# First tiles of seven normed products taken from x·A before the rstd is known, and one sum instead of four behind the post-norms

## Chip, cores, metric

One Trainium2 chip, one of its cores. The metric is device time in microseconds (us) of one execution. The engines: TensorE (PE in the profile; PEld is its weight load), VectorE (DVE), ScalarE (ACT), GpSimd (POOL) and SyncE (SP), on whose queue nearly all DMAs are issued.

## What is computed

Two model blocks in float32, one after the other, each of two layers, on 256 tokens of 1024 features; block 1 also carries 256 tokens of context through its first layer.

```python
# block 1, layer l (x and the context cx alike; cx is not updated in layer 1)
sh1, sc1, ga1, sh2, sc2, ga2 = split(silu(c) @ w_mod + b_mod, 6)
u = (rmsnorm(x, g_mix) * (1 + sc1) + sh1) @ w_in      # pool | linear attention | attention
x = x + ga1 * (concat([pool, gla, attention]) @ w_out)
x = x + ga2 * (square(relu((rmsnorm(x, g_mlp) * (1 + sc2) + sh2) @ w_up)) @ w_down)
# after both layers: x = rmsnorm(x, g_final)

# block 2, layer l
shift_a, scale_a, gate_a, shift_f, scale_f, gate_f = split(silu(c) @ w_ada + b_ada, 6)
h = rmsnorm(x, g_mix_pre) * (1 + scale_a) + shift_a
x = x + gate_a * rmsnorm(hybrid_mixer(h), g_mix_post)  # three attentions, then @ w_out
h = rmsnorm(x, g_ffn_pre) * (1 + scale_f) + shift_f
x = x + gate_f * rmsnorm((silu(h @ w_gate) * (h @ w_up)) @ w_down, g_ffn_post)
```

rmsnorm multiplies a token by the inverse root of its mean square (the rstd) and by a gain.

## The kernel before

Activations lie with the features on the partitions: `x` is eight tiles ("chunks") of 128 features by 512 columns. In block 1 these are the 256 tokens and the 256 context tokens (T = 512; 256 in layer 1 behind the in-projection); in block 2 the tokens take the first 256 columns and the output `y` of a mixer or feed-forward the others.

**Products.** Every weight is streamed once, in pieces `wraw` (two buffers) on SP's queue. ACT casts a piece to a rounded part `whi` (L135), DVE subtracts to get the rest `wlo` (L136); activations are split in the same way. An output tile of 128 features is a sum of three matmuls a chunk (high by high, high by low, low by high), so a 1024-deep tile is 24 matmuls and a pair of tiles 48. A product is written with one tile after the other, or `by_k`, chunk by chunk over all its tiles, so that it can follow a norm that delivers chunk after chunk. For the first products behind a norm the weights are split ahead (`early`, and `early_act` for two more tiles, `wact`).

**A norm.** ACT squares the chunks, DVE or POOL adds the squares, TensorE sums over the partitions (`st`, matmuls with ones), DVE makes the mean (`ms`, L236), POOL raises it to −1/2 (L237), TensorE transposes the rstd onto all partitions (`bc`). Then `norm_chunk` makes each h chunk: DVE `nt` = x·A·rstd (L295), ACT adds B and rounds (L297, L299), DVE, ACT or POOL make the low part (L300 to L303). A and B come from the modulation vectors.

**Post (block 2).** Behind w_out and behind the feed-forward of layer 0, x + G·r·y is normed at once. `Post.chunk` gathers four sums as the y tiles arrive: of x², of x·G·y, of (G·y)² and of y², with three ACT squares, a DVE product (L1229), a DVE add of 512 columns (L1231) and a POOL add of 512 columns (L1232, DVE for the last tile). Two `pow` steps then give both rstds, one `bc` holds them, and `Post.norm` updates x and makes h. `first_norm` does the like between the blocks.

**Fill.** The modulation vectors are products of their own: 24 or 32 matmuls `pmod` from eight `mraw` DMAs of 512 KB each. `queue_mod` queues them and `pump` emits steps (one DMA, four matmuls, which the profile counts as eight) at a given `pace` per product; a scheduler that orders each engine's instructions ahead of the run puts them where it expects TensorE to wait. `mraw` has two buffers in layer 0 of block 1, four in layer 1, six in block 2. SP's queue is served in order: a DMA that waits for a buffer holds up those behind it.

Of the kernel before, what the change touches and what calls it, by code (L numbers as in the profile page):

```python
# [10 lines left out]
F32 = mybir.dt.float32  # L11
# [9 lines left out]
D = 1024  # L21
# [3 lines left out]
LAG, ADDV, TAIL = 1, (1, 3, 5, 7), 6  # L25
PACE1 = 2, 1
# [4 lines left out]
class K:  # L31
# [6 lines left out]
    # ---------------------------------------------------------------- pools  # L38
# [91 lines left out]
    # ------------------------------------------------------- building blocks  # L130
# [18 lines left out]
    def gemm_a(self, src, nt, h, t0, t1, evac, by_k=False):  # L149
        """src [128, nt*K*128]: output features on partitions, tokens t0:t1 of the chunks h."""  # L150
# [27 lines left out]

    def gemm_half(self, src, h, half, t0, t1, evac):
        """gemm_a for two tiles, over one half of the chunks of h."""  # L180
# [15 lines left out]
    def early(self, src, nt, K_):  # L196
        """The weights of the next product by chunks, ahead of what comes before it."""
# [5 lines left out]
    def early_act(self, src, act):  # L203
        """Two tiles more, kept where the activations are."""
# [7 lines left out]
    def gemm_b(self, src, N, h, tts, evac):  # L212
        """src [128, K*N]: tokens on partitions, one output per token tile of tts."""
# [6 lines left out]
        for tt in tts:  # L220
            t = slice(tt * 128, (tt + 1) * 128)
            p = self.psum("pb")
            o = p[:, :N]
            for k in range(K_):
                hi, lo = gr[k // g]
                w = slice((k % g) * N, (k % g + 1) * N)
                self.mm(o, h[k][:, 0, t], hi[:, w], k == 0, False)
                self.mm(o, h[k][:, 0, t], lo[:, w], False, False)
                self.mm(o, h[k][:, 1, t], hi[:, w], False, k == K_ - 1)
            evac(tt, o)  # L230

    def pow_rstd(self, dst, st, n, tag="smn"):
        """dst = (st / n + eps) ** -0.5"""
# [5 lines left out]
    def exp_rstd(self, dst, st, n, tag="smn"):  # L239
        """The same for many columns, where the table of Exp and Ln is loaded: a step of Newton's makes it exact."""  # L240
# [10 lines left out]
    def rstd_bc(self, groups, T, sets=(6, 1, 1), eng=None):  # L251
# [4 lines left out]
        st = self.psum("st")  # L256
# [22 lines left out]
        bc = self.psum("bc")  # L279
# [4 lines left out]
    def norm_mod(self, T, mod, act, *sets, bc=None):  # L284
        """mod: [(t0, t1, A [128,8], B [128,8])]; the chunks of x * rstd * A + B, split."""
# [20 lines left out]
    def modulation(self, b, l, ss, boot=None):  # L306
        """The vectors ss of layer l of block b, [128, rows, 8] each, a row block of the weights a step."""
# [29 lines left out]
    def pump(self, n=None):  # L337
        """Emit n steps of the queued modulations (all of them: None)."""
# [13 lines left out]
    def gain(self, g, sc, tag):  # L352
        """g * (1 + sc)"""
# [4 lines left out]
    # ---------------------------------------------------------------- block 1  # L358
    def block1(self, top):
        tc, nc, a = self.tc, self.nc, self.a  # L360
        ranges = [(0, 256), (256, 512)]
        for l in range(2):
            T = 512 if l == 0 else 256
            m = lambda s: self.mod(0, l, s)
            with ExitStack() as es:
                self.mrp = es.enter_context(tc.tile_pool(name=f"mrp{l}", bufs=(2, 4)[l], reuse_waits="tile"))
                act = es.enter_context(tc.tile_pool(name=f"act{l}", bufs=10, reuse_waits="tile"))
                if l == 0:
# [7 lines left out]
                else:  # L376
                    self.early(a["w_in_a"][1, 0], 2, 8)
# [3 lines left out]
                h = self.norm_mod(512, [(*ranges[r], A[r], m(0)[:, r]) for r in range(2)], act)  # L381
                with tc.tile_pool(name=f"mix{l}", bufs=1, reuse_waits="tile") as mp:
                    self.queue_mod(0, l, [2, 3, 4], PACE1[l])
                    mix = self.mixers1(l, T, h, act, mp)
# [1034 lines left out]
```

## Time and profile before

| | |
|---|---|
| three executions | 1909.71, 1912.74, 1915.86 us (median 1912.74) |
| profiled execution | span 1926.9 us from its first to its last instruction |
| TensorE busy | 1822.9 us, 95% of the span |
| DVE, ACT, POOL busy | 1077.5, 816.9, 226.9 us |
| mean granted TensorE clock | 0.959 |

The profile is of an execution of its own; its span is already 14.2 us (0.7%) above the median of the others, and it has no time beside the span that the views show. All views below are of that one execution, in us from its first instruction. TensorE's busy time counts overlapping matmuls once, but it also counts fill and matmuls at a low clock as busy.

### The profile page before, as it was taken

What the parts mean: (1) busy time and instruction counts of PE and PEld (TensorE: products, weight loads), DVE (VectorE), ACT (ScalarE), POOL (GpSimd) and SP (SyncE); (2) the same over time, 40 slices, a digit from 0 to 9 for tenths busy, and PEclk for the clock granted to TensorE, in tenths of its full rate; (3) what the DMA queues carried; (4) which work ended last, traced back from release to release, by engine and by line L of the source; (5) the groups of instructions that cost most, each with busy time, mean ns of one, the idle gap of its engine ahead of it and who ended that gap; (6) DMA issues with size and microseconds to landing.
All of it is one profiled execution on the core that took longest, in us unless ns stands there. A gap on an engine that the chain in (4) does not pass through costs nothing. (4 is left out here: it accounts for less than half of the span.)

```text
span 1926.9 us, 31942 instructions
## 1 busy us (share of the span) xinstructions
PE 1822.9 (95%) x12982; PEld 1509.5 (78%) x12982; DVE 1077.5 (56%) x2012; ACT 816.9 (42%) x1563; POOL 226.9 (12%) x253
## 2 busy tenths in 40 slices
PE   5998799999999999989999999998999899989998
PEld 3776446778777787865799986986999868869997
DVE  3237865544444546277666564466544754575555
ACT  3343433433222224544454444464444445544443
POOL 2024410100000002051100012012000230030000
PEclk9998978999999999999999998997999989989999
DMA  8422321232333234424655676345666654254553
GB/s 324 165 90 77 122 84 34 99 109 88 120 131 113 106 131 151 162 94 138 214 206 193 212 262 224 111 127 191 205 212 218 208 200 168 78 175 163 187 177 130
DMA packets 66211, 298.75 MB, mean 155 GB/s; under 512 B 9552, under 2 KB 13572, under 8 KB 45328
## 3 DMA queue, kind: packets, MB, share of 16 engines
q1 hardware_dynamic: 65168, 295.65, 45.0%
q8 instruction: 102, 1.67, 0.3%
q0 software_dynamic: 464, 1.05, 0.2%
q14 instruction: 45, 0.37, 0.1%
q10 hardware_dynamic: 432, 0.01, 0.0%
HBM read 295.63 MB, written 1.05 MB: 154 GB/s over the span
## 5 line engine op out<-in xcount | busy, mean ns | idle before, releaser
L132 PE MATMUL pa<-h,whi 128*128 128x256 f32 (+1 forms) x3008 | 660.6, 315 | 10.5 <-ACT h L299 9.3
L136 DVE TENSOR_TENSOR wlo<-wraw,whi 128x1024 fp32r<-128x1024 f32 (+4 forms) x406 | 448.4, 1105 | 365.6 <-ACT whi L135 362.5
L135 ACT CAST whi<-wraw 128x1024 fp32r<-128x1024 f32 (+4 forms) x406 | 380.3, 937 | 608.1 <-PE pa L132 576.7
L132 PEld LDWEIGHTS pa<-h,whi 128*128 128x128 f32 x3008 | 496.0, 192 | 61.3 <-ACT h L299 11.9
L132 PE MATMUL pa<-h,wlo 128*128 128x256 f32 (+1 forms) x1504 | 469.8, 312 | 0.0
L132 PE MATMUL pa<-hid,whi 128*128 128x256 f32 (+1 forms) x1728 | 381.4, 317 | 0.3
L132 PEld LDWEIGHTS pa<-hid,whi 128*128 128x128 f32 x1728 | 284.1, 190 | 29.4 <-issue 4.1
L132 PEld LDWEIGHTS pa<-h,wlo 128*128 128x128 f32 x1504 | 289.4, 192 | 18.4 <-DVE wlo L136 1.2
L132 PE MATMUL pa<-hid,wlo 128*128 128x256 f32 (+1 forms) x864 | 273.4, 316 | 2.3 <-DVE wlo L136 2.3
L132 PEld LDWEIGHTS pa<-hid,wlo 128*128 128x128 f32 x864 | 163.8, 190 | 14.5 <-DVE wlo L136 3.2
L392 DVE SCALAR_TENSOR_TENSOR x<-pa,mod,x 128x256 f32<-128x256 f32 x184 | 82.3, 479 | 109.0 <-PE pa L132 108.9
L132 PE MATMUL pmod<-mraw,cp 128*32 128x256 f32 x1408 | 135.0, 412 | 2.8 <-DMA mraw<-in_w_mod_dram 2.2
L132 PE MATMUL pa<-mixc,whi 128*128 128x256 f32 (+1 forms) x512 | 118.6, 321 | 1.9 <-ACT sq L1228 1.9
L132 PEld LDWEIGHTS pa<-mixc,whi 128*128 128x128 f32 x512 | 84.3, 190 | 18.7 <-issue 3.8
L132 PE MATMUL pb<-whi,h 128*128 128x256 f32 (+2 forms) x480 | 98.2, 296 | 0.0
L132 PEld LDWEIGHTS pb<-whi,h 128*128 128x128 f32 x480 | 78.1, 193 | 6.4 <-issue 4.6
L132 PE MATMUL pa<-mixc,wlo 128*128 128x256 f32 (+1 forms) x256 | 80.7, 318 | 0.0
L132 PEld LDWEIGHTS pmod<-mraw,cp 128*32 128x32 f32 x1408 | 39.4, 112 | 48.1 <-issue 22.9
L132 PE MATMUL pb<-wlo,h 128*128 128x256 f32 (+2 forms) x240 | 70.7, 296 | 0.2 <-DVE wlo L136 0.2
L824 DVE TENSOR_REDUCE mx<-pS 128x1 f32<-128x512 f32 (+3 forms) x80 | 45.4, 578 | 37.6 <-PE pS L132 37.3
L135 ACT CAST hid<-rsq 128x512 fp32r<-128x512 f32 (+1 forms) x64 | 32.9, 513 | 71.3 <-DVE rsq L432 71.1
L1232 POOL TENSOR_TENSOR acc<-acc,sq 128x512 f32<-128x512 f32 x18 | 28.4, 1577 | 221.5 <-DVE sq L1229 218.8
(327 smaller groups left out, 2099.3 us busy)
## 6 DMA issues: line engine op xcount, KB each, us to landing
mraw<-in_w_ada_dram SPq DMA_DIRECT2D x96, 512.0 KB, 5.2
wraw<-in_w_gate_up_dram SPq DMA_DIRECT2D x44, 1024.0 KB, 4.9
mraw<-in_w_mod_dram SPq DMA_DIRECT2D x80, 512.0 KB, 4.1
wraw<-in_w_up_dram SPq DMA_DIRECT2D x32, 1024.0 KB, 5.0
wraw<-in_w_down_dram SPq DMA_DIRECT2D x32, 1024.0 KB, 5.0
wraw<-in_w_down_2a_dram SPq DMA_DIRECT2D x16, 1024.0 KB, 5.2
wraw<-in_w_in_2a_dram SPq DMA_DIRECT2D x12, 1024.0 KB, 5.0
wraw<-in_w_in_a_dram SPq DMA_DIRECT2D x10, 1024.0 KB, 7.4
```

Of the source, the lines that this page charges most:

```text
L132: self.last = self.nc.tensor.matmul(out, l, r, start=start, stop=stop, **k).ins
L135: self.nc.scalar.copy(hi, src)
L136: self.nc.vector.tensor_sub(lo, src, hi)
L392: nc.vector.scalar_tensor_tensor(self.x[n][:, s], o[:, s], gate()[:, r, n:n + 1], self.x[n][:, s], op0=ALU.mult, op1=ALU.add)
L824: nc.vector.reduce_max(mx, s, axis=AX.X)
L1232: (nc.vector if k == 7 else nc.gpsimd).tensor_add(self.acc[1], self.acc[1], b)
```

## The change

Seven norms (all but the first of block 1 and the last of block 2) now feed their first tiles twice over. `Lead` makes `xa`, the split of x·A without the rstd, with B as a 257th column (and a column of zeros). `Kernel.lead` multiplies the first two tiles (block 1) or four (block 2) by `xa`, 258 columns wide. The rstd comes later: `lead_out` copies column 256 (W·B) as a bias, multiplies the rest in PSUM by `rr`, the rstd on all partitions, and ACT adds the bias. The remaining tiles still use h, made as before, so the next product becomes the `by_k` one (`i == 1` in the MLP, `i == 2` in the feed-forward, w_in_r in layer 1 of block 1).

`Post` gathers the squares of y alone. x is updated by `update` as soon as that rstd is there, and the norm behind it takes its squares from the new x (`norm`, added up on POOL).

The modulations are queued in another order and at other paces, and `mraw` has three buffers instead of four in layer 1 of block 1.

```diff
-PACE1 = 2, 1
+PACE1 = 3.4, 2.4
...
+    def lead(self, xa, n, by_k=False):
...
+        order = [2, 3, 0, 1][-n:]
+        o = {}
+        for i, j in enumerate(order):
+            o[j] = [self.psum("pS" if i * R + r < 2 else "pa") for r in range(R)]
+        if by_k:
+            steps = [(k, j) for k in range(8) for j in order]
+        else:
+            steps = [(k, j) for j in order for k in range(7)] + [(7, j) for j in order]
...
+            for r in range(R):
+                p = o[j][r][:, :258]
+                self.mm(p, hi, xa[r][:, k, 0], k == 0, False)
+                self.mm(p, hi, xa[r][:, k, 1], False, False)
+                self.mm(p, lo, xa[r][:, k, 0], False, k == 7)
...
+    def lead_out(self, p, rr, dst):
...
+        b = self.small(1, "lb", "smgl")
+        self.nc.vector.tensor_copy(b, p[:, 256:257])
+        self.nc.vector.tensor_mul(dst, p[:, :256], rr)
+        return b
...
-                self.mrp = es.enter_context(tc.tile_pool(name=f"mrp{l}", bufs=(2, 4)[l], reuse_waits="tile"))
+                self.mrp = es.enter_context(tc.tile_pool(name=f"mrp{l}", bufs=(2, 3)[l], reuse_waits="tile"))
...
+            if g == 0:
+                for p in lead:
+                    r = self.etmp(T, "relu")
+                    for i, q in enumerate(p):
+                        t = r[:, i * 256:(i + 1) * 256]
+                        b = self.lead_out(q, rr[:, i * 256:(i + 1) * 256], t)
+                        nc.scalar.activation(t, t, AF.Relu, bias=b)
+                    square(r, hs)
+                h.extend(self.norm_mod(T, mods, act, bc=bc))
...
-        self.gemm_b(a["w_in_r"][l], 288, h, range(4), lambda tt, o: nc.scalar.copy(rkv[:, tt], o))
+        self.gemm_b(a["w_in_r"][l], 288, h, range(4), lambda tt, o: nc.scalar.copy(rkv[:, tt], o), by_k=bool(lead))
...
+                    if f:
+                        f.rstd()
+                    for k in range(8):
+                        if f:
+                            f.update(k)
+                        lead.chunk(k)
+                    return self.lead(lead.xa, 4, by_k=f is not None)
...
+            def norm(mods):
+                bc = self.rstd_bc([(xs, D)], 256, eng=nc.gpsimd, bank="pqt")
+                return bc[:, :256], lambda: self.norm_mod(256, mods, act, bc=bc)
...
+                self.queue_mod(1, l, [2, 3, 4], 1.7)
...
-                    self.queue_mod(1, l, [2])
-                    self.pump()
...
-                self.queue_mod(1, l, [3, 4])
...
-                    self.queue_mod(1, 1, [0, 1], 0.6)
+                    self.queue_mod(1, 1, [0, 1], 0.9)
...
+    def chunk(self, k):
+        nc = self.K.nc
+        for c, (t0, t1, A, _) in zip(self.xa, self.mods):
+            x, g = self.K.x[k][:, t0:t1], A[:, k:k + 1]
+            nc.scalar.activation(c[:, k, 0, :256], x, AF.Copy, scale=g)
+            nc.vector.scalar_tensor_tensor(c[:, k, 1, :256], x, g, c[:, k, 0, :256], op0=ALU.mult, op1=ALU.subtract)
...
-        nc.scalar.activation(b[:, :256], x, AF.Square)
-        nc.scalar.activation(c[:, 256:], y, AF.Square)
-        nc.scalar.activation(c[:, :256], y, AF.Square, scale=G)
-        nc.vector.scalar_tensor_tensor(b[:, 256:], y, G, x, op0=ALU.mult, op1=ALU.mult)
-        if 0 < k < TAIL + 1:
-            nc.vector.tensor_add(self.acc[0], self.acc[0], c)
-            (nc.vector if k == 7 else nc.gpsimd).tensor_add(self.acc[1], self.acc[1], b)
...
+        nc.scalar.activation(q, self.y[k], AF.Square)
+        if k == 0:
+            self.acc = q
+        elif k < 6:
+            nc.vector.tensor_add(self.acc, self.acc, q)
```

How the order of instructions moves is shown at three places; the rows are those of the program, with the counts of its own matmuls (a `pmod` of the program is two in the profile).

First, TensorE at the feed-forward's norm in layer 0 of block 2, before the change: from the last matmul of w_out (`pa<-mixc`) to the first of the feed-forward (`pa<-h`, `pS<-h,wact`).

```order
L132 MATMUL pa<-mixc,wlo 128x256
L132 MATMUL pmod<-mraw,cp_83 32x256 x19
L132 MATMUL st<-ones,acc 128x1 x8
L132 MATMUL pmod<-mraw,cp_83 32x256 x4
L132 MATMUL st<-ones,sq 128x1 x8
L132 MATMUL pmod<-mraw,cp_83 32x256 x4
L1254 MATMUL bc<-c_ident,r_12237 128x128 x4
L132 MATMUL pa<-h,whi 128x256 x2
L132 MATMUL pS<-h,wact 128x256 x2
```

With the change, the same place: to the first matmuls with `xa`, and then from the last of those (row `pqt` on) to the first with h.

```order
L132 MATMUL pa<-mixc,wlo 128x256
L132 MATMUL st<-ones,sq 128x1 x2
L132 MATMUL pmod<-mraw,cp_83 32x256 x7
L359 MATMUL pmt<-c_ident,modr 128x128 x2
L132 MATMUL st<-ones,sq 128x1 x2
L132 MATMUL pmod<-mraw,cp_83 32x256 x20
L1369 MATMUL bc<-c_ident,r_12492 128x128 x2
L132 MATMUL pmod<-mraw,cp_83 32x256 x4
L132 MATMUL pS<-xa_12487,wact 128x258 x2
L132 MATMUL pa<-xa_12487,whi 128x258 x2
```

```order
L132 MATMUL pa<-xa_12487,wlo 128x258
L132 MATMUL pqt<-ones,sq 128x1 x6
L132 MATMUL pmod<-mraw,cp_83 32x256 x4
L316 MATMUL pqt<-c_ident,rs 128x128 x2
L132 MATMUL pmod<-mraw,cp_83 32x256 x3
L359 MATMUL pmt<-c_ident,modr 128x128 x2
L132 MATMUL pmod<-mraw,cp_83 32x256 x20
L132 MATMUL pa<-h,whi 128x256 x2
```

One wait with 27 program matmuls of fill has become two, with 31 and 27; the 96 matmuls with `xa` stand between them, and the sums of the new norm (`pqt`) stand behind the last of them.

Second, DVE at the first norm of block 2 with the change, from the scaling of the first tiles (`cq`, `ck`, L210) to the inputs of the attention's next product (`lt`, `lat`).

```order
L210 TENSOR_TENSOR cq<-pa,rr 128x256 x2
L210 TENSOR_TENSOR ck<-pS,rr 128x256 x2
L330 SCALAR_TENSOR_TENSOR nt<-x,A_10509,bc 128x256 x3
L335 SCALAR_TENSOR_TENSOR h<-nt,mod_8327,h 128x256
L330 SCALAR_TENSOR_TENSOR nt<-x,A_10509,bc 128x256 x3
L335 SCALAR_TENSOR_TENSOR h<-nt,mod_8327,h 128x256
L330 SCALAR_TENSOR_TENSOR nt<-x,A_10509,bc 128x256
...
L335 SCALAR_TENSOR_TENSOR h<-nt,mod_8327,h 128x256
L1060 SCALAR_TENSOR_TENSOR x<-x,c_g_final,bc 128x256 x8
L271 TENSOR_SCALAR ms<-st 128x2 x2
L1166 SCALAR_TENSOR_TENSOR lt<-cq,c_g_q_lat,st 128x256 x2
L1166 SCALAR_TENSOR_TENSOR lt<-ck,c_g_kv_lat,st 128x256
```

The same place before, from the last two h chunks on (L295 and L300 make h, L963 updates x):

```order
L300 SCALAR_TENSOR_TENSOR h<-nt,mod_9194,h 128x256
L295 SCALAR_TENSOR_TENSOR nt<-x,A_10288,bc 128x256
L963 SCALAR_TENSOR_TENSOR x<-x,c_g_final,bc 128x256
L300 SCALAR_TENSOR_TENSOR h<-nt,mod_9194,h 128x256
L963 SCALAR_TENSOR_TENSOR x<-x,c_g_final,bc 128x256 x7
L1209 TENSOR_TENSOR pg<-c_g_mix_post,mod_11868 128x8
L136 TENSOR_TENSOR wlo<-wraw,whi 128x128 x2
L236 TENSOR_SCALAR ms<-st 128x2 x2
L1047 SCALAR_TENSOR_TENSOR lt<-cq,c_g_q_lat,bc 128x256 x2
L1047 SCALAR_TENSOR_TENSOR lt<-ck,c_g_kv_lat,bc 128x256
```

There `cq` and `ck` are written by ACT, and the h chunks and updates of x stand ahead of the product whose tiles they are; now all of them stand between the scaling of those tiles and `ms`, which the next product waits for.

Third, TensorE in layer 1 of block 1 with the change, from the end of w_in_r (`pS<-whi,h`) over the gates of the linear attention (`pg`, from `rkv` over `rT` to `la`) to the next in-projection tiles (`pa<-h`).

```order
L132 MATMUL pS<-whi,h 128x288
L675 MATMUL pg<-c_ident,rkv 32x128 x4
L132 MATMUL pmod<-mraw,cp_82 32x256 x4
L132 MATMUL pg<-wg,rT 128x512
L132 MATMUL pmod<-mraw,cp_82 32x256 x8
L132 MATMUL pg<-wg,rT 128x512
L132 MATMUL pmod<-mraw,cp_82 32x256 x4
L359 MATMUL pmt<-c_ident,modr 128x128 x2
L132 MATMUL pg<-c_UF,la 128x256
L132 MATMUL pg<-c_UF,la 128x128
L132 MATMUL pg<-c_UF,la 128x256
L132 MATMUL pa<-h,whi 128x256 x2
```

Before, the two in-projections `pa<-h` (96 matmuls) came straight behind w_in_r, with `pg<-c_ident,rkv` behind them:

```order
L132 MATMUL pb<-whi,h 128x288 x2
L132 MATMUL pb<-wlo,h 128x288
L132 MATMUL pb<-whi,h 128x288
L132 MATMUL pmod<-mraw,cp_82 32x256 x4
L132 MATMUL pa<-h,whi 128x256 x2
...
L132 MATMUL pa<-h,wlo 128x256
L132 MATMUL pa<-h,whi 128x256 x2
L132 MATMUL pa<-h,wlo 128x256
L600 MATMUL pg<-c_ident,rkv 32x128 x4
L132 MATMUL pmod<-mraw,cp_82 32x256 x4
L132 MATMUL pb<-whi,h 128x256
```

So 96 matmuls that covered the way from `rkv` to `la` now stand behind it.

## Rows read from the trace of the kernel before

**Rows 1.** The page, part 1: busy time, share, instructions.

```profile
PE 1822.9 (95%) x12982; PEld 1509.5 (78%) x12982; DVE 1077.5 (56%) x2012; ACT 816.9 (42%) x1563; POOL 226.9 (12%) x253
```

**Rows 2.** Windows, each from a product's end: PE, PEld, DVE, ACT, POOL, PEclk, DMA.

```profile
740.60:763.20 22.60, 20.71 (x128) 14.13 (x126) 13.77 (x28) 11.52 (x23) 9.09 (x11) 0.92 0.48 174
763.20:779.40 16.20, 16.18 (x130) 13.99 (x128) 3.59 (x6) 4.92 (x8) 0.00 (x0) 1.00 0.71 260
947.60:960.70 13.10, 11.92 (x106) 8.82 (x104) 7.17 (x15) 7.09 (x16) 5.13 (x8) 1.00 0.85 307
1147.00:1183.80 36.80, 34.18 (x274) 23.74 (x272) 17.89 (x49) 16.47 (x40) 6.50 (x9) 0.86 0.57 202
1306.00:1341.30 35.30, 27.27 (x188) 23.19 (x187) 21.04 (x49) 13.59 (x33) 10.28 (x12) 0.71 0.50 184
1537.70:1578.60 40.90, 35.79 (x282) 25.82 (x281) 22.56 (x59) 17.08 (x42) 12.20 (x15) 0.83 0.55 197
1701.10:1735.20 34.10, 25.88 (x188) 22.03 (x186) 21.01 (x49) 13.01 (x31) 10.30 (x12) 0.75 0.32 111
```

**Rows 3.** Of the same windows, the fill (tile pmod) alone.

```profile
1306.00:1341.30 35.30, 4.69 (x54) 1.48 (x54) 0.00 (x0) 0.71 0.50 184
1537.70:1578.60 40.90, 13.67 (x128) 4.49 (x128) 0.83 (x2) 0.83 0.55 197
```

**Rows 4.** Timeline of PE, feed-forward norm of block 2, layer 0: start, us.

```profile
1306.15 2.54 PE L132 MATMUL pmod<-mraw,cp 128*32 128x256 f32 x38
1313.15 3.58 PE L132 MATMUL st<-ones,acc 128*128 128x1 f32 x16 [4.47 <-DVE acc L1231]
1317.67 3.57 PE L132 MATMUL st<-ones,sq 128*128 128x1 f32 x16
1327.15 0.79 PE L132 MATMUL pa<-h,whi 128*128 128x256 f32 x2 [2.43 <-ACT h L299]
```

**Rows 5.** The chain that ended last: start, us, piece.

```profile
1329.23 0.85 PE pS L132 x4
1334.38 0.72 PE pa L132 x6
1383.68 0.57 PE pmod L132 x8
1515.38 4.52 PE pa L132 x36
1562.96 0.72 PE pa L132 x6
1737.82 177.84 PE pa L132 x1482
```

**Rows 6.** Timeline of DVE around three norms.

```profile
1167.92 2.82 DVE L963 SCALAR_TENSOR_TENSOR x<-x,c_g_final,bc 128x256 f32<-128x256 f32 x7
1289.32 1.23 DVE L136 TENSOR_TENSOR wlo<-wraw,whi 128x1024 fp32r<-128x1024 f32 x1 [0.46 <-ACT whi L135]
1296.32 1.45 DVE L1231 TENSOR_TENSOR acc<-acc,sq 128x512 f32<-128x512 f32 x1
1313.42 2.76 DVE L136 TENSOR_TENSOR wact<-wraw,wact 128x256 fp32r<-128x256 f32 x8
1326.08 0.48 DVE L295 SCALAR_TENSOR_TENSOR nt<-x,A,bc 128x256 f32<-128x256 f32 x1 [0.45 <-POOL x L1261]
```

**Rows 7.** Timeline of POOL there.

```profile
1321.52 0.71 POOL L237 TENSOR_TENSOR r<-ms,mhalf 128x2 f32<-128x2 f32 x1 [10.10 <-DVE ms L236]
```

**Rows 8.** Timeline of ACT and DVE, gates of the linear attention, layer 1 of block 1.

```profile
797.27 0.72 ACT L588 ACTIVATE lsg<-lsg,ones 128x512 f32<-128x512 f32 x1
798.03 0.69 DVE L589 SCALAR_TENSOR_TENSOR la<-pg,lsg 128x512 f32<-128x512 f32 x1 [2.60 <-ACT lsg L588]
```

**Rows 9.** Windows as in group 2, mixers of that layer.

```profile
820.00:840.00 20.00, 16.03 (x127) 13.65 (x125) 16.02 (x36) 9.72 (x21) 9.97 (x13) 1.00 0.47 158
```

**Rows 10.** DMA issues between 735 and 800: count, KB, median us to landing.

```profile
mraw<-in_w_mod_dram SPq DMA_DIRECT2D x13, 512.0 KB, 4.7
```

More of the change, by code (lines that the diff above doesn't have):

```diff
@@ L24 @@
 EPS = 1e-6
-LAG, ADDV, TAIL = 1, (1, 3, 5, 7), 6
-PACE1 = 2, 1
+ADDV = 1, 3, 5, 7
+PACE1 = 3.4, 2.4
 GAN = 1152
@@ L396, in block1, with res, ev @@
-                    ev = res(lambda: m(2))
+                self.pump()
+                A = [self.gain(self.g_mlp[:, l], m(4)[:, r], f"A2{r}") for r in range(2)]
+                mods = [(*ranges[r], A[r], m(3)[:, r]) for r in range(T // 256)]
+                def res(gate, lead=None):
+                    def ev(n, o):
+                        for r in range(T // 256):
+                            s = slice(r * 256, r * 256 + 256)
+                            nc.vector.scalar_tensor_tensor(self.x[n][:, s], o[:, s], gate()[:, r, n:n + 1], self.x[n][:, s],
+                                                           op0=ALU.mult, op1=ALU.add)
+                        if lead:
+                            lead.chunk(n)
+                    return ev
@@ L397, in block1 @@
+                with tc.tile_pool(name=f"xup{l}", bufs=1, reuse_waits="tile") as xp:
+                    lead = Lead(self, xp, mods)
+                    ev = res(lambda: m(2), lead)
                     for i in range(4):
@@ L399, in block1 @@
                     del mix
[L400 to L403 removed]
+                    self.early(a["w_up"][l, 0], 2, 8)
+                    o = self.lead(lead.xa, 2)
                 ev = res(lambda: m(5))
@@ L1024, in ffn, with mixers2 @@
         if l == 0:
-            f = Post(self, y, self.f_post[:, l], self.mod(1, l, 5)[:, 0])
+            f = Post(self, y)
         down(2)
         return f
-    def mixers2(self, l, h, act, mp, y):
+    def mixers2(self, l, lead, norm, act, mp, y):
         nc, a = self.nc, self.a
@@ L1037, in mixers2 @@
         ckv, kr = ck[:, 0], ck[:, 1]
-        self.gemm_a(None, 2, h, 0, 256, lambda j, o: nc.scalar.copy((cq if j < 2 else ck)[:, j % 2], o), by_k=True)
+        b2, rest = norm()
+        rr = self.lv(mp, 256, "rr")
+        nc.scalar.copy(rr, b2)
+        for j, p in enumerate(lead):
+            t = (cq if j < 2 else ck)[:, j % 2]
+            b = self.lead_out(p[0], rr, t)
+            nc.scalar.activation(t, t, AF.Identity, bias=b)
+        h = rest()
         mix = [act.tile([128, 2, 256], F32R, name="mixc", tag="act") for _ in range(8)]
@@ L1201, with __init__ @@
 class Post:
[L1205 removed]
+    def __init__(self, K, y):
         self.K, self.y = K, y
[L1207 to L1209 removed]
         self.st = K.psum("st")
[L1211 to L1220 removed]
@@ L1241, in norm @@
[L1241 to L1264 removed]
+        self.acc = None
@@ new lines, in chunk @@
+    def chunk(self, k):
+        K, nc = self.K, self.K.nc
+        q = K.tp.tile([128, 512], F32, name="sq", tag="sq" if k else "ssq", bufs=2)[:, :256]
+        nc.scalar.activation(q, self.y[k], AF.Square)
[3 more added lines that the diff above has]
+            nc.vector.tensor_add(self.acc, self.acc, q)
+        if k >= 5:
+            s = self.acc if k == 5 else q
+            for i in range(2):
+                K.mm(self.st[:, i:i + 1], s[:, i * 128:(i + 1) * 128], K.ones[:, :1], k == 5 and i == 0, k == 7, skip_group_check=True)
@@ new lines, in rstd, with gain, update @@
+    def rstd(self):
+        K, nc = self.K, self.K.nc
+        r = K.small(2, "r1")
+        K.pow_rstd(r, self.st[:, 0:2], D)
+        self.bc = K.psum("bc")
+        for i in range(2):
+            nc.tensor.transpose(self.bc[:, i * 128:(i + 1) * 128], r[:, i:i + 1].to_broadcast([128, 128]), K.ident)
+    def gain(self, g, gate):
+        self.G = self.K.modp.tile([128, 8], F32, name="pg", tag="pg", bufs=2)
+        self.K.nc.vector.tensor_mul(self.G, g, gate)
+    def update(self, k):
+        K, nc = self.K, self.K.nc
+        t = K.tmp(256, "post")
+        x = K.x[k][:, :256]
+        nc.vector.scalar_tensor_tensor(t, self.y[k], self.G[:, k:k + 1], self.bc[:, :256], op0=ALU.mult, op1=ALU.mult)
+        (nc.vector if k in ADDV else nc.gpsimd).tensor_add(x, x, t)
```

228 lines of the change are left out of this document (121 added, 107 removed).

## Prediction, made before the changed kernel ran

> **What bounds the kernel now.** The page comes first: TensorE is busy for 95% of the span [rows 1], so time is won only where it waits, runs at half clock, or does work that could lie in a wait. Windows over the norms show these places [rows 2]: from the end of one product until the tiles behind the norm are done, 35.3 us at a mean clock of 0.71 in the feed-forward of layer 0, 34.1 in layer 1, 40.9 and 36.8 at block 2's mixers, 22.6 and 13.1 in layer 1 of block 1. The timeline of one says why [rows 4]: w_out is done at 1306.0, fill lasts until 1308.7, then TensorE waits 4.47 us for a sum on DVE, sums at half clock, and has its first h only at 1327.15. The chain of waits shows two more costs: fill that stands in a stream that never waits (a step is a piece of 0.57 us, as at 1383.68), and the half clock, 1.2 instead of 2.4 GHz, at which four matmuls take 0.85 us where six later take 0.72 [rows 5].
>
> **The change part by part.** Below, t is us from the end of the product ahead of a norm, and a matmul is 0.12 us, from 1482 in 177.84 [rows 5].
>
> *Fill.* I counted program matmuls of fill in both orders, four to a step. In the streams behind the first tiles of the two MLPs and feed-forwards 37 steps stand before (11, 9, 16, 1), about 3 now; the first in-projection has 8 more. The rest has gone into waits: 26 x 0.57 = **14.8 us** less. Bounds: nothing, if the waits grow by what they take in, and 21 if the in-projection hides its 8.
>
> *Post's sums.* In layer 0's last w_down, DVE's adds of 512 columns take up to 1.45 us beside POOL's [rows 6] and hold up `wlo`. The chain's stream holds 1374 matmuls from 1344.09 on until it breaks at 1519.9 (16 pieces of them, the last is shown); the same stream in layer 1 is 1482 [rows 5]. The other 108 should take 13.0 us and take 17.8, to 1537.7: **4.8 us**, which one 256-column add a tile gives back.
>
> *Feed-forward norms.* At the end of w_out DVE has `wlo` (1.23) and then eight `wact` pieces (2.76) ahead of `ms` [rows 6]: `ms` at t = 5.4, `pow` 0.71 [rows 7], `bc` at 7.2, then three post products, POOL's add, one `xa`: first matmul about 9.4. The 96 wide ones take 11.7, and 2 for a half-clock start: 23. The sums of the new norm stand behind them: sums, `ms`, `pow`, transposes, copy, four scalings and the first h on DVE at 0.48 each [rows 6], about 7, so h at 30. Its 48 matmuls are paced by h chunks at 1.0 us: 38.4. Before, those 48 came after the 96 at full rate: 35.3 + 5.8 = 41.1 and 39.9 [rows 2]. **2.7 and 1.5 us** less: a wait of 21 us is replaced by two, of 9 and 7. Bounds per norm: 6 less (h not late) and 4 more (each gap ends at half clock).
>
> *Second mixer of block 2.* `xa` starts at t = 7.2 and the 96 matmuls end at 21. Then come the rstd, four scalings, eight chunks of h on DVE (twelve operations of 0.48 and a `modr`), and only then `ms` and the chain to the next product: 16 us, in which before half lay under the matmuls. First matmul at 37 against 40.9 [rows 2]: **3.9 less**.
>
> *First norm of block 2.* The same with 2.82 us for seven of the eight x updates in the way [rows 6], two rstds, and `xa` behind all of `wlo` and `wact`: about 42 against 36.8 [rows 2]: **5.2 more**. Bounds for these two together: 8 less, 12 more.
>
> *Layer 1 of block 1, MLP norm.* x·A is made as w_out's tiles leave, so the first 48 matmuls (5.8) follow w_out at once; a chain of 5 and 48 matmuls paced by h follow, 17.5 against 13.1 + 5.8 [rows 2]: **1.5 less**. The MLP norm of layer 0 gains its wait and pays one like it: nothing, 2 either way.
>
> *Layer 1 of block 1, in-projection.* Here I expect a loss. `xa` starts behind `wlo` and small operations at t = 4.5; the first tile is paced by 14 products of 0.48 on DVE, the second by TensorE, so the lead ends near 17.7 and h is there near 25. w_in_r by chunks has 96 matmuls (12.8 us) and 11 steps of fill. With three buffers and 4.7 us from a DMA's issue to landing [rows 10], three steps take 5.3 us, 1.77 each: 19.5 us, to 44.5. Before, w_in_r ends at 38.8 (22.6 + 16.2) and 96 matmuls of in-projection follow, so that the way to the gates is covered. Now that way is bare: copies and transposes 2.5, then twice a product, three activations of some 0.65 and `la` 0.69 [rows 8], near 6: the in-projection starts at 53.5, 15 us later. What is given back is the later wait for the same gates: the mixers of this layer leave TensorE idle for 4.0 us of 820 to 840 [rows 9], and for more behind it, and the 96 matmuls can fill that. I take 8 back: **7 more**, with bounds of 0 and 15.
>
> The sum: 14.8 + 4.8 + 2.7 + 1.5 + 3.9 + 1.5 - 5.2 - 7 = 17.0 less. It is made in the profiled execution, whose span of 1926.9 is 0.7% above the median of the runs; the difference carries over unscaled within 0.2 us: 1912.7 - 17 = **1896 us**.
>
> *The clock.* A gap with plenty of fill need not end slow: in the second mixer's norm, 128 fill records stand in the stretch [rows 3], and six matmuls of its product take 0.72 at 1562.96 [rows 5]; in the feed-forward's, with 54 records, four take 0.85 at 1329.23. The change makes two gaps of each one, and the second in layer 1's feed-forward has no fill left at all. The Trainium skill ("TensorE: Matmul & The Clock Gate", section "HAM oscillation — how this bites in real kernels") says that bursts of matmuls with waits between them are throttled anew, each burst starting slow, which speaks against two gaps. The traces agree for gaps with little fill. By that rule alone every second gap would end slow, and the sum would be that of the third rival.
>
> **Rivals.**
> First, *the gain is larger*: the in-projection's late start is given back in full (7), block 2's first norm breaks even (5), and the second waits are as short as their bare chains (about 6). For it: the mixers of block 1 do wait later [rows 9]. Against: on DVE the order is fixed, and the scalings and h stand ahead of `ms`. 1896 - 18 = 1878.
>
> Second, *slower*: fill that arrives late. In layer 1 of block 1 all 24 steps now stand before the in-projection, on three buffers, with 18 of their DMAs in a row on SP ahead of the next weights. If each one of the 15 or so behind the lead is waited for at its landing and weights then take as long again, the in-projection comes not 15 but 30 us late, and block 2's first norm, with 45 program matmuls of fill together there, another 10. It decides once these two places lose over 29 us, against the 12 that I take: 1912.7 + about 10 = 1923. For it: SP's order, and the landing time [rows 10]. Against: block 2 has six buffers, and the wait on the gates hides some of these DMAs.
>
> Third, *nearly no change*: every norm's second gap costs its half-clock start. Between the pieces at 1329.23 and 1334.38 [rows 5] that is 5.15 us at 0.21 instead of 0.12 a matmul, 2.2 lost; seven times that is 15, and 17 - 15 leaves 2: about 1911. For it: layer 1's feed-forward. Against: the other gaps keep 20 or more matmuls of fill.
>
> **How the numbers follow.** My sum 0.47, with its own range of 1886 to 1906; larger gain 0.2; no change 0.15; slower 0.18. Three runs before lie 0.3% apart, so that is what a measurement can tell: under 1907 is faster, over 1918.5 slower. Faster 0.47 + 0.2 and a little of the third, 0.69; same 0.14; slower 0.17. For 8 in 10 the range leaves out a little of either end: 1870 (the bounds of all gains) to 1917.
>
> **What would show each step.** Right: no POOL adds of 512 columns and no 4.47 us wait behind w_out; unbroken streams of 1482 matmuls in both feed-forwards; two gaps a norm in block 2, near 9 and 7 us; matmuls with `xa` at 0.12. In layer 1 of block 1, TensorE idle between w_in_r and the in-projection, and fuller than before 40 us on. Wrong: `wlo` or `wact` late for the lead, fill waited for at its DMA, a second gap over 12 us, or the in-projection over 20 us later than before with the idle time behind it unchanged.

## The result, and the profile of the changed kernel

The changed kernel takes 1930.42 us (median of four runs, 1928.42 to 1937.16) beside 1913.88 us for the kernel before on the same chip: a ratio of 1.010, with a 95% interval of 1.0069 to 1.013. It is slower by 1%, where 1896 us was forecast; the time lies outside the range (1870 to 1917), on the side of the second rival.

The execution that the prediction read was itself a long one. A second profile of the kernel before (`before_again`) has a span of 1914.3 us; it lacks a half-clock stretch in layer 0's mixers that costs the first 18 us. All stages below are compared with the second; the sum of the prediction does not rest on that stretch.

The page of the changed kernel, parts 1 and 4:

```profile
PE 1800.7 (93%) x13054; PEld 1496.9 (78%) x13054; DVE 1094.3 (57%) x2118; ACT 840.9 (44%) x1622; POOL 232.9 (12%) x265
...
PE 77%; DVE 7%; DMA 5%; POOL 2%; ACT 2%; issue 1%; SPq 0%; ACTq 0%; POOLq 0%; DVEq 0%
```

Over the whole, TensorE is busy for less time than before [rows 1] and the kernel takes longer: the loss is waiting. 5% of the chain that ended last are DMAs.

Windows of five stages, first `before_again`, then the changed kernel (columns as in [rows 2]): layer 0 of block 1 from the end of w_out to the first w_down tile; layer 1 from there to the end of its w_out; layer 1's MLP from its first w_down tile on; layer 0 of block 2 to the end of w_out; its feed-forward from the first w_down tile on.

```profile
344.96:401.13 56.17, 53.60 (x262) 40.87 (x260) 30.63 (x49) 25.50 (x43) 6.21 (x5) 0.97 0.35 122
...
722.56:928.48 205.92, 194.31 (x1560) 144.31 (x1558) 127.72 (x263) 95.58 (x183) 47.27 (x51) 0.97 0.44 148
...
984.09:1129.56 145.47, 144.71 (x1231) 139.46 (x1230) 91.49 (x125) 66.17 (x98) 5.23 (x6) 1.00 0.63 216
1129.56:1288.90 159.34, 152.78 (x1194) 125.65 (x1197) 87.30 (x211) 84.61 (x225) 22.58 (x27) 0.97 0.49 166
...
1409.37:1519.38 110.01, 107.37 (x904) 100.57 (x906) 62.17 (x78) 47.56 (x74) 9.07 (x5) 1.00 0.64 206
```

```profile
348.04:410.89 62.85, 57.16 (x318) 44.30 (x316) 33.12 (x59) 27.36 (x48) 7.12 (x5) 0.89 0.34 118
...
725.14:952.80 227.66, 204.93 (x1671) 151.36 (x1672) 141.68 (x303) 105.92 (x209) 57.07 (x61) 0.93 0.45 154
...
1014.79:1152.09 137.30, 137.30 (x1155) 137.12 (x1154) 90.45 (x120) 65.76 (x98) 5.22 (x6) 1.00 0.59 208
1152.09:1320.27 168.18, 158.29 (x1245) 126.74 (x1244) 88.71 (x233) 85.29 (x225) 16.60 (x23) 0.95 0.50 176
...
1439.33:1538.59 99.26, 99.23 (x830) 98.89 (x832) 55.35 (x70) 44.31 (x65) 0.00 (x0) 1.00 0.53 182
```

The streams gain as planned: 8.2 us in the MLP and 10.8 us in the feed-forward, with TensorE busy throughout. Two stages lose more: layer 1 of block 1 takes 227.66 instead of 205.92 us (21.7 more, of which TensorE is idle for 11.1 and busy for 10.6, at a lower mean clock and with eight more steps of fill, 320 records instead of 256), and block 2's first mixers 8.8 more. The norm of the first MLP loses 6.7.

The fill (tile `pmod`) alone, from the view of one tile: how long TensorE and its weight loads stood idle ahead of it and what ended that, as us and times. A wait can count for both queues, so these are for comparing kernels, not for adding up. First `before_again`, then the changed kernel:

```profile
  DMA mraw<-in_w_mod_dram: 7.4, 10
...
  DMA mraw<-in_w_ada_dram: 4.6, 6
```

```profile
  DMA mraw<-in_w_mod_dram: 37.0, 33
...
  DMA mraw<-in_w_ada_dram: 24.6, 23
```

12 us of waiting for fill's weights have become 62, as both queues count it; for the matmuls alone it is 4.0 and 23.9. The chain of waits of the changed kernel shows where, in layer 1 of block 1 (start, us, piece):

```profile
744.43 3.94 DMA mraw<-in_w_mod_dram
748.42 0.79 PE pmod L132 x8
749.21 1.74 PE pb L132 x6
...
753.66 6.29 DMA mraw<-in_w_mod_dram
...
768.46 4.74 DMA mraw<-in_w_mod_dram
...
775.88 6.38 DMA mraw<-in_w_mod_dram
782.30 1.12 PE pmod L132 x8
```

The four DMA pieces are 21.4 us, but that is the way by which the last work was released, and TensorE was not idle for so long: while these weights were on their way it did earlier steps of fill and matmuls of w_in_r between them. Its timeline shows what it waited itself, in brackets:

```profile
748.42 0.79 PE L132 MATMUL pmod<-mraw,cp 128*32 128x256 f32 x8 [2.37 <-DMA mraw<-in_w_mod_dram]
759.99 0.64 PE L132 MATMUL pmod<-mraw,cp 128*32 128x256 f32 x8 [1.27 <-DMA mraw<-in_w_mod_dram]
773.24 0.64 PE L132 MATMUL pmod<-mraw,cp 128*32 128x256 f32 x8 [0.21 <-DMA mraw<-in_w_mod_dram]
782.30 1.08 PE L132 MATMUL pmod<-mraw,cp 128*32 128x256 f32 x8 [0.20 <-DMA mraw<-in_w_mod_dram]
```

In the whole layer it stood 6.9 us ahead of fill for its DMAs, at 7 of 40 steps (1.4 us at one before). w_in_r (`pb`, `pS`) stands in order behind the first three of these and goes on without a wait of its own.

The timeline of SP's queue there (start, us, DMAs in a row), `before_again` and then the changed kernel:

```profile
744.90 0.33 SPq L314 DMA_DIRECT2D mraw<-in_w_mod_dram  x1
745.96 0.33 SPq L140 DMA_DIRECT2D wraw<-in_w_in_a_dram  x1
746.38 0.38 SPq L314 DMA_DIRECT2D mraw<-in_w_mod_dram  x1
747.98 0.33 SPq L140 DMA_DIRECT2D wraw<-in_w_in_a_dram  x1
749.23 11.91 SPq L314 DMA_DIRECT2D mraw<-in_w_mod_dram  x3
```

```profile
741.37 34.83 SPq L349 DMA_DIRECT2D mraw<-in_w_mod_dram  x18
776.26 0.90 SPq L140 DMA_DIRECT2D wraw<-in_w_in_a_dram  x2
```

Before, the weights of the in-projection were called for between single DMAs of fill, 745.96 - 722.56 = 23.4 us into the layer. Now 18 DMAs on three buffers stand ahead of them, and they are called for at 776.26 - 725.14 = 51.1 us. The first in-projection behind w_in_r in `before_again`, and then in the changed kernel the cast that waits for these weights and the in-projection:

```profile
760.68 0.51 PE L132 MATMUL pa<-h,whi 128*128 128x256 f32 x2
```

```profile
784.72 1.99 ACT L135 CAST whi<-wraw 128x1024 fp32r<-128x1024 f32 x2 [0.57 <-DMA wraw<-in_w_in_a_dram]
787.69 0.99 PE L132 MATMUL pa<-h,whi 128*128 128x256 f32 x2
```

So the weights are there 59.6 us into the layer, and the in-projection starts at 62.6 us instead of 38.1.

### The profile page after: what moved, and what is told of

Same layout as the page of the kernel before. It is cut to its first block, busy times and chain, and to the rows that moved or that the text cites. A ratio compares the mean times of both kernels' runs of the same rounds, so it can differ in the third digit from the quotient of the medians.

```text
span 1926.8 us, 32255 instructions
## 1 busy us (share of the span) xinstructions
PE 1800.7 (93%) x13054; PEld 1496.9 (78%) x13054; DVE 1094.3 (57%) x2118; ACT 840.9 (44%) x1622; POOL 232.9 (12%) x265
## 4 chain that ended last, share of the span: by engine, by line
PE 77%; DVE 7%; DMA 5%; POOL 2%; ACT 2%; issue 1%; SPq 0%; ACTq 0%; POOLq 0%; DVEq 0%
PE pa L132 56%; PE pS L132 6%; PE pmod L132 3%; PE pO L132 3%; PE pb L132 2%; PE pg L132 2%; DMA mraw<-in_w_mod_dram 2%; DMA mraw<-in_w_ada_dram 2%; DVE Qz L748 1%; DVE wlo L136 1%; PE pPT L875 1%; PE st L132 1%; ACT whi L135 1%; PE pPT L1286 1%; POOL rs L272 1%
## 5 line engine op out<-in xcount | busy, mean ns | idle before, releaser
L136 DVE TENSOR_TENSOR wlo<-wraw,whi 128x1024 fp32r<-128x1024 f32 (+4 forms) x406 | 442.7, 1092 | 323.8 <-ACT whi L135 321.2
L132 PE MATMUL pa<-h,whi 128*128 128x256 f32 (+1 forms) x2784 | 606.4, 314 | 8.2 <-ACT h L334 6.2
L132 PEld LDWEIGHTS pa<-h,whi 128*128 128x128 f32 x2784 | 459.6, 193 | 48.7 <-ACT h L334 7.4
L132 PE MATMUL pa<-h,wlo 128*128 128x256 f32 (+1 forms) x1392 | 435.4, 313 | 1.4 <-DVE wlo L136 1.4
L132 PEld LDWEIGHTS pa<-h,wlo 128*128 128x128 f32 x1392 | 268.1, 193 | 20.5 <-DVE wlo L136 3.9
L132 PE MATMUL pb<-whi,h 128*128 128x256 f32 (+2 forms) x448 | 92.7, 297 | 0.0
L305 POOL TENSOR_TENSOR sq<-sq 128x256 f32<-128x256 f32 (+1 forms) x30 | 30.5, 1017 | 431.8 <-ACT sq L301 429.0
L132 PEld LDWEIGHTS pb<-whi,h 128*128 128x128 f32 x448 | 73.2, 194 | 7.1 <-issue 5.9
L132 PE MATMUL pb<-wlo,h 128*128 128x256 f32 (+2 forms) x224 | 66.1, 295 | 0.0
```

The source lines that it names most:

```text
L132: self.last = self.nc.tensor.matmul(out, l, r, start=start, stop=stop, **k).ins
L136: self.nc.vector.tensor_sub(lo, src, hi)
L305: (eng or nc.vector).tensor_add(s, s, q)
```

## The experiments

Two theories. **A**: the fill costs. It was put earlier, in a quick row on few buffers; TensorE waits in order for each of its DMAs, and SP issues them ahead of the next weights. **B**: the leads cost. Each replaces a covered way by two bare chains (rstd, scaling in PSUM, activation, next product). Every ratio is against the kernel before on the same chip. In the stage times, "to w_out" is from the end of the last w_down to the end of w_out.

**before_again.** The kernel before, unchanged, profiled again.

> The kernel before once more, unchanged, for a second profile: the trace that the prediction was made from has a span of 1926.9 us, while the other executions took 1910 to 1916. If the trace was one slow execution, this one has a span near 1912 and lacks the half-clock stretch between 270 and 305 (w_out of block 1, layer 0 starts near 311 instead of 325). If profiling itself costs 14 us, the span is near 1927 again, and then the changed kernel's trace, 1926.8 at 1928.6 us, should have been longer too.

1916.04 us, span 1914.3. It gives the stages used above.

**in_proj_by_h.** The changed kernel, with the lead of layer 1's in-projection undone:

```diff
...
-                    with tc.tile_pool(name="xin", bufs=1, reuse_waits="tile") as xp:
-                        lead = Lead(self, xp, mods)
...
-                        o = self.lead(lead.xa, 2)
+                h = self.norm_mod(512, mods, act)
```

> The changed kernel, but the in-projection of layer 1 in block 1 is as before (h made from the rstd, w_in_r tile after tile). Theory A (the loss lies at this place and at block 2's first norm, where fill waits for its DMAs): from w_down's end to the in-projection's first h 39 us instead of 62.5, some 3 us given back in the mixers, so about 20 us less than the changed kernel, near 1910. Theory B (the doubled waits of all seven norms cost a little each, this place no more than the others): 3 to 5 us less, near 1926.

1924.88 us, ratio 1.0054 (1.0007 to 1.0102). The layer takes 222.8 us to w_out, 5 less than with the lead and 17 more than before, and SP still has 17 DMAs of fill in one row. So 5 us went with the lead, and the rest of what the layer had lost stayed, its in-projection at 62.5 us too. The time is the one put beside B; the 1910 us put beside A are missed, since the row of fill did not go away with the lead. What that row costs by itself had to be tried apart.

**resident_fill_after, resident_fill_before.** In both kernels the products of fill take one resident tile; their DMAs are left out, all but those of the start, so that the modulation vectors are other numbers.

```diff
-                w = boot.tile([128, 1024], F32, name="mboot") if boot else self.mrp.tile([128, 1024], F32, name="mraw")
-                nc.sync.dma_start(w, self.a[name][l, k * 128:(k + 1) * 128, s * 1024:(s + 1) * 1024])
+                w = boot.tile([128, 1024], F32, name="mboot") if boot else self.mres
```

> The changed kernel with the modulation products reading one resident tile: their 160-odd DMAs of 512 KB are left out, so the modulations are wrong; all matmuls stay. Theory A (fill waits for its DMAs on TensorE, in order, and holds up what stands behind it): the stretch before layer 1's in-projection falls from 62.5 to 45 to 48, block 2's first norm from 46 to about 38, and the whole is 25 to 35 us shorter, near 1900. Theory B (the chains from the lead over the scaling on DVE to the next product are bare, whatever the fill does): both stretches fall by less than 4 us, the whole by less than 10.

> The same edit on the kernel before: modulation products from one resident tile, their DMAs left out. Its trace shows few waits for these DMAs, so both theories expect 3 to 10 us less than before, near 1906. What tells them apart is the distance to the changed kernel with the same edit: theory A says that one is then some 5 to 15 us faster than this, theory B that it is still 10 us or more slower.

1896.74 us (ratio 0.9892, 0.9863 to 0.9921) and 1889.84 us (0.9862, 0.984 to 0.9884). Against 1930.42 (on another chip) and 1915.16 us with all their DMAs that is 33.7 and 25.3 us less. For the changed kernel that is what A expected; for the kernel before it is far more than the 3 to 10 us that both theories expected, so fill's DMAs cost that kernel too. Without them layer 1 takes 211.4 and 207.7 us to w_out: 18 of the 22 us are gone. But the edit also moves the fill (in the changed kernel 26 records of it stand within w_in_r instead of 96, and none in block 2's second mixer), so this pair does not tell waits from places. And the change is still 6.9 us behind the kernel before, between the two expectations and nearer to B's (10 or more): some of the leads may cost too.

**pace_only.** The changed kernel with the old rate of fill:

```diff
-PACE1 = 3.4, 2.4
+PACE1 = 2, 1
```

> The changed kernel with the old rate of fill in block 1's mixers (PACE1 back to 2, 1), so that 9 instead of 18 mraw DMAs stand in a row on SP ahead of the next in-projection's weights; three buffers and all leads stay. Theory A (fill that stands earlier waits for its DMAs and makes TensorE wait in order): layer 1 of block 1, to the end of w_out, falls from 227.7 us to about 214, the whole from 1929 to about 1916. Theory B (the chains laid bare behind each lead cost, not the fill): 227.7 stays within 3 us and the time within 3 of 1929.

1919.6 us, ratio 0.9997 (0.9974 to 1.002). Layer 1's window and SP's queue in it:

```profile
724.06:937.85 213.79, 196.96 (x1653) 148.99 (x1654) 138.95 (x301) 105.87 (x209) 55.55 (x61) 0.97 0.48 159
```

```profile
740.29 18.81 SPq L349 DMA_DIRECT2D mraw<-in_w_mod_dram  x9
759.16 0.42 SPq L140 DMA_DIRECT2D wraw<-in_w_in_a_dram  x1
```

As A expected, 213.8 and not 227.7: 13.9 us back, with the lead and the three buffers still there, and an in-projection that starts at 45.8 us. The whole is 4 us over A's 1916.

**proj_h_pace_buf4.** pace_only, with the in-projection by h as in in_proj_by_h and `bufs=(2, 4)[l]`.

> The in-projection of layer 1 of block 1 by h as before, PACE1 back to 2, 1, and four mraw buffers in that layer: this layer's mixers are then those of the kernel before. Theory A: to the end of w_out 206 to 209 us (227.7 with the change, 222.8 with the in-projection by h alone), the whole about 1910, which is 14 less than with the in-projection by h alone. Theory B: the in-projection by h already took away what the lead cost, so this is within 3 us of 1925.

1913.71 us, ratio 0.9982 (0.9959 to 1.0005): the total A expected within 4 us, but not its 206 to 209 us for the layer. That takes 214.1 us, just as with the lead and three buffers, so at this rate that lead and the buffer together cost nothing there. 8 us against before remain.

**both_h_pace_buf4.** Also block 2's first norm by h:

```diff
-                    o = first(a["w_in_2a"][0], mods)
-                    stats = lambda: self.first_norm(mods, act)
+                    self.early(a["w_in_2a"][0, 0], 2, 8)
+                    self.early_act(a["w_in_2a"][0, 1], act)
+                    h0 = self.first_norm(mods, act)[1]()
+                    o = None
+                    stats = lambda: (None, h0)
...
```

> As the run before, and block 2's first norm by h as before too; leads are left in the two MLP norms, the two feed-forward norms and the second mixer of block 2. Theory A: layer 0 of block 2 goes from 168 us (to the end of w_out) to about 160, since its fill stands behind the norm again, the whole about 1902. Theory B gives about 4 of these 8 us, 1906 or 1921 by what the run before gives.

1907.36 us, ratio 0.9955 (0.9926 to 0.9985). Its layer 0 of block 2 took 163.8 us to w_out in the profile, nearer to what B gives than to A's 160; the three kernels below, with the same first norm, took 159.2, 160.6 and 161.4, and those with the lead at this point 168.2, 164.2, 165.9 and 166.6. The means differ by 5.0 us; in the pair without fill's DMAs (159.4 and 156.8) it is 2.6, though these two differ in Post's sums and in the place of fill too.

**block2_leads.** Also the two MLP norms by h (`ev = res(lambda: m(2))`, `h.extend(self.norm_mod(T, mods, act))` and the first up product `by_k`, as before).

> As the run before, and the two MLP norms of block 1 by h as before; leads are left in the two feed-forward norms and the second mixer of block 2, with the single sum. From the end of w_out to the first w_down tile of the MLPs took 62.9 and 62.0 us with the change and 56.2 and 55.6 before, while the rest of the MLP took 7 and 8 less. If the lead itself costs there (B), these two fall by 6 us each and the rest keeps its gain: 10 us less than the run before, about 1892. If what is lost there is the same fill work, only moved (A), the two sums stay and the time is within 3 us of the run before.

1899.55 us, ratio 0.99 (0.9866 to 0.9935): the fastest kernel of the study with all its work done, 1% faster than before. From w_out to the first w_down tile the MLPs took 62.4 and 57.8 us with the lead and 56.8 and 55.9 without, and what follows stayed at 319.7 and 138 us. Here B holds: the leads of the MLPs cost 5.6 and 1.9 us, where 6 each had been expected, and the whole is 7.8 us less. In layer 0 the trace puts most of it on fill once more: with the lead, in both_h_pace_buf4, TensorE stands 3.7 us of the norm for fill's DMAs, without it not at all. The step in the second gap there:

```profile
371.56 1.08 PE L132 MATMUL pmod<-mraw,cp 128*32 128x256 f32 x8 [3.18 <-DMA mraw<-in_w_mod_dram]
```

**one_sum_only.** The kernel before with the changed `Post`, no leads:

```diff
...
+        f.gain(g, gate)
+        f.rstd()
+        for k in range(8):
+            f.update(k)
+        return self.norm_mod(256, [(0, 256, A, B)], act, bc=self.rstd_bc([([x[:, :256] for x in self.x], D)], 256, eng=self.nc.gpsimd))
```

> The kernel before with the changed Post alone: one sum (of y) is gathered over w_down and w_out, x is updated, and the norm that follows sums x in a second chain with nothing but fill to cover it; no leads. If the prediction's price for Post's sums holds, layer 0's last w_down of block 2 takes 4.8 us less, and the feed-forward stretch 105 us in place of 110. Theory B: the second chain without a lead then adds some 9 us at each of the three norms behind a Post, so that the time is 1930 to 1940 beside 1916. A rival: fill covers the second chain, and the time is about 1911.

1910.35 us, ratio 0.999 (0.9956 to 1.0024): the rival holds. From w_out to the first w_down tile takes 122.9 and 119.0 us in the feed-forwards beside 120.5 and 116.3, so the second chain costs about 2.5 us a norm, not 9. And the last w_down gains only 1.8 (108.23 from 110.01). TensorE's waits in that stage, `before_again` and then this kernel (us in total, times, longest):

```profile
PE pa L132 <- DVE wlo L136: 2.3, 3, 1.1
```

```profile
PE st L132 <- ACT sq L1219: 1.0, 1, 1.0
```

The waits for `wlo` are gone, as planned, but they were 2.3 us and not 4.8.

**ffn_by_h.** block2_leads, with the feed-forward norms by h behind the single sum; one lead is left.

> The kernel with leads in block 2 alone (1900 us), and the two feed-forward norms by h as well, behind the second chain; the one lead left is that of block 2's second mixer. If the leads of the feed-forward norms are worth what they were made for, 96 matmuls of 0.12 us (11.5 us) stood in a wait and now stand behind it: 119 and 117 us from the end of w_out to the first w_down tile become about 129 and 127, the whole 1915 to 1922. If those leads cost as much as they cover, as the MLP's did, the time is 1895 to 1903.

1904.36 us, ratio 0.9949 (0.9926 to 0.9972): between the two, 5 us behind block2_leads (which ran on another chip; the ratios differ by 0.5%). By one profile of each, the lead saves 5.8 us in layer 0 (124.9 to 119.1), where fill is at hand, and loses 1.4 in layer 1 (115.4 to 116.8), where there is almost none.

**fast_fill_before.** The kernel before, with nothing of the change but these two lines:

```diff
-PACE1 = 2, 1
+PACE1 = 3.4, 2.4
...
-                self.mrp = es.enter_context(tc.tile_pool(name=f"mrp{l}", bufs=(2, 4)[l], reuse_waits="tile"))
+                self.mrp = es.enter_context(tc.tile_pool(name=f"mrp{l}", bufs=(2, 3)[l], reuse_waits="tile"))
```

> The kernel before with nothing but the changed rate of fill in block 1's mixers (PACE1 3.4, 2.4) and its three buffers in layer 1 instead of four; no lead, no single sum. If the late fill alone is what costs (theory A), layer 1 of block 1 to the end of w_out goes from 206 us to 218 to 224, the whole from 1915 to about 1928, as slow as the changed kernel. If the leads' bare chains are needed for the loss (theory B), 206 stays within 3 us and the time is 1912 to 1918.

1926.6 us, ratio 1.0044 (1.0019 to 1.0069). The window of layer 1 to w_out, and SP's queue:

```profile
731.69:957.86 226.17, 206.16 (x1625) 148.20 (x1624) 129.70 (x265) 95.48 (x183) 49.93 (x53) 0.92 0.47 153
```

```profile
744.75 38.12 SPq L314 DMA_DIRECT2D mraw<-in_w_mod_dram  x17
782.92 0.90 SPq L140 DMA_DIRECT2D wraw<-in_w_in_a_dram  x2
```

Without a single lead, the layer loses 20.3 us, its in-projection starts at 61.7 us, and the gains in the streams come too (321.4 to 315.0, 145.5 to 137.6, 110.0 to 102.0). Of the last, 7.6 us come back in the feed-forward norm ahead of it (120.5 to 128.1), into which 88 records of fill went. This settles A for the largest loss. Its size is less sure: the profiled execution, 1932.86 us, was the longest of the twelve, and in_proj_by_h, the other kernel with this fill and without this lead, lost 16.9 there. What no run tells apart: how much TensorE's waits for fill cost and how much the late weights, and what the third buffer alone does at this rate.

**leads2_early_w.** block2_leads, with `early` for layer 1's in-projection ahead of the pumped fill again, as before.

> The kernel with leads in block 2 alone (1900 us), with the weights of layer 1's in-projection called for ahead of the pumped fill again, as in the kernel before, instead of behind it. That layer of block 1 took 214 us to the end of w_out, 8 more than before, though its in-projection is by h, its fill at the old rate and its buffers four. If these weights behind six mraw DMAs on SP are the cause, 214 becomes about 208 and the whole about 1894. If the cause is the 13 steps of fill that stand ahead of w_out now and behind it before, 214 stays and so do 1900 us.

1902.54 us, ratio 0.9929 (0.9903 to 0.9955), and 215.7 us in layer 1: no gain. The 8 us that the layer keeps at the old rate would then be the fill that stands ahead of w_out now and stood behind it before: 320 records instead of 256, with 8 left in the MLP instead of 72. No run has put it back, so this is not shown. It is not a loss of the whole: the MLP behind it takes 7 us less.

## Why the prediction was wrong, step by step

| step | forecast, us | measured, changed kernel against `before_again` | the edit by itself |
|---|---|---|---|
| fill out of the streams | -14.8 | -7.2, -8.2, and the larger part of -10.8 | -6.4, -7.8, -8.0 (fast_fill_before), but +7.6 in the feed-forward norm ahead of the last |
| Post's sums | -4.8 | the rest of the -10.8 | -1.8 (one_sum_only); -2.7 (102.00 to 99.26, the fill gone in both) |
| feed-forward norms | -2.7, -1.5 | -1.4, +0.2 | lead: -5.8, +1.4 (ffn_by_h) |
| second mixer of block 2 | -3.9 | -6.9 to the end of w_out (half-clock stretch before); -0.5 at its first product (40.6 to 40.1) | |
| first norm of block 2 | +5.2 | +8.8 | lead: +5 (four kernels each); +2.6 in the pair without DMAs of fill, not the lead alone |
| MLP norm, layer 1 | -1.5 | +6.4 | lead: +1.9 |
| MLP norm, layer 0 | 0 (2 either way) | +6.7 | lead: +5.6 |
| layer 1's in-projection | +7 (0 to 15) | +21.7 | lead and buffer at the old rate: 0; fill: +20.3 (+16.9 in in_proj_by_h) |

With 3.1 more in layer 0's mixers, the middle column (-6.9 for the second mixer) adds up to the 12.5 us between the spans. Those 6.9 us are mostly a half-clock stretch of `before_again`: the first profile of the kernel before has 163.5 us there, the changed kernel 162.4.

**The step that failed** is "Layer 1 of block 1, in-projection", with its counterpart, "Bounds: nothing, if the waits grow by what they take in". w_in_r starts at t = 24.0, near the 25 forecast, but ends at 49.3 and not 44.5, and the in-projection starts at 62.6 and not 53.5 (38.1 before): 24 us late, not 15. Of that I gave 8 back, for later waits that the delay would cover; the rest of the layer gives back 2.7 (165.1 instead of 167.8 us). Of the 15 us, 9 were charged to the lead's bare way to the gates, the rest to the fill within w_in_r. The runs show that the fill makes most of it: without the lead the in-projection still starts at 61.7 and 62.5 (fast_fill_before, in_proj_by_h), with the lead and the old rate at 45.8 (pace_only, where it follows w_in_r at once, as before), and the fill alone costs 20.3 of the 21.7 us (16.9 in in_proj_by_h). The sum had no term for SP's order, by which the in-projection's weights come behind 18 DMAs of fill. The streams themselves gained what they were to gain (34 steps of 0.57 us are 19.4; fast_fill_before has 22), but the bound of "nothing" was no bound: the waits grew by more than they took in.

The second rival had this mechanism, SP's 18 DMAs and its point of decision, 29 us lost in two places. The two places lost 21.7 + 8.8 = 30.5, and the time is on its side, 1930 instead of 1923. Its detail is not all borne out: TensorE waits at the landing of 7 of the layer's 40 steps, not of 15 or so. I gave it 0.18 against my 0.47 because "block 2 has six buffers, and the wait on the gates hides some of these DMAs". The gates were little cover: the weights landed 59.6 us into the layer, 6 us behind the time at which my sum has the in-projection start.

**What was right.** The two gaps of the feed-forward norm. TensorE in layer 1's, changed kernel, start, us and the wait ahead (it answers to [rows 4], there of layer 0); w_out ends at 1700.94:

```profile
1707.21 0.69 PE L1369 MATMUL bc<-c_ident,r 128*128 128x128 f32 x2 [3.52 <-POOL r L272]
1709.82 0.80 PE L132 MATMUL pS<-xa,wact 128*128 128x258 f32 x2 [1.92 <-ACT xa L1338]
...
1723.62 1.39 PE L132 MATMUL pqt<-ones,sq 128*128 128x1 f32 x12
1727.03 0.43 PE L316 MATMUL pqt<-c_ident,rs 128*128 128x128 f32 x2 [2.01 <-POOL rs L272]
1730.70 1.17 PE L132 MATMUL pa<-h,whi 128*128 128x256 f32 x3 [3.24 <-ACT h L334]
1731.68 0.41 PE L132 MATMUL pa<-h,wlo 128*128 128x256 f32 x1
1731.89 0.41 PE L132 MATMUL pa<-h,whi 128*128 128x256 f32 x1
1732.10 0.41 PE L132 MATMUL pa<-h,wlo 128*128 128x256 f32 x1
```

The first wide matmul comes at t = 8.9 (9.4 forecast), the lead ends at 22.7 (23), h is there at 29.8 (30). And still nothing is saved: behind the second gap the h matmuls follow one another every 0.21 us, half the rate, up to 1738, so the tiles are done at 39.8 and not 38.4. That is the third rival's mechanism, in the norm it named. The Trainium skill ("TensorE: Matmul & The Clock Gate", "HAM oscillation — how this bites in real kernels") says of a kernel with a long wait after each burst of matmuls that every burst starts throttled; this trace agrees here, and so do the mean clocks of the stages with more waits, 0.93 for 0.97 in layer 1 and 0.89 for 0.97 in layer 0's MLP norm. It does not for every doubled gap: from w_out to the first w_down tile in layer 0 of block 2, where fill stands in both gaps, the mean clock rose from 0.91 to 0.96.

**Where a size was off.** *MLP norm, layer 0*: I set this to nothing, and the lead costs 5.6. Its 96 matmuls are half as wide as the 48 that they stand for (0.12 and 0.23 us each), so they are no more work; the second gap waits 3.7 us for fill's DMAs. *MLP norm, layer 1*: the lead costs 1.9 where I had 1.5 less; the rest went when the rate of fill and then in-projection and buffers were put back (62.0, 59.8, 57.5 us). *Second mixer*: the lead ended at 21.5 as forecast (21), but the way behind it, counted as 16 us, took 18.6; 2.6 of these are one wait for a DMA of fill. *Post's sums*: of the 4.8 us by which the last 108 matmuls were slow, TensorE waited only 2.3 for `wlo`; one_sum_only gains 1.8. *First norm of block 2* was priced rightly for the lead (5.2 forecast, 5 between four kernels each); what else makes up the 8.8, fill in the gap or the difference between executions, no run tells apart.

## What to carry to other kernels

Fill in a wait was not free here when its own data came late or when it held up other weights: before moving it, follow its DMAs, count its buffers, and see what it pushes back on the queue that issues it. Deferring the rstd paid where fill covered the second chain (5.8 us in layer 0's feed-forward) and cost where the second gap was bare or waited for fill's DMAs (1.4 to 5.6 us). In a chain of waits, a DMA piece is no idle time: ask the busy engine's own timeline what it waited. Test the parts of such a bundle one by one: with three of the seven leads, the single sum and the old rate of fill, the kernel is 1% faster than before instead of 1% slower.

## What was not expected of the hardware

A step of fill in a stream that never waits costs more than its matmuls: nine steps left layer 0's and layer 1's MLP streams (88 records of fill to 16, and 72 to none), which got 7.2 and 8.2 us shorter, 0.8 to 0.9 a step, where a piece in the chain is 0.57; where the rest goes, no run shows. And executions of one kernel differ by a half-clock stretch in a mixer, at no fixed place: layer 0's took 362.9 and 345.0 us to w_out in the two profiles of the kernel before, and those of layer 1 of block 2 163.5 and 169.3.
